# Dividing three early loads of a DMA-bound transpose into pieces of 112, 8 and 8 partitions

## The chip, the cores and the metric

One core of one Trainium2 chip. The metric is the device time of one execution in microseconds, and less is better. All runs told here are of the fast or undisturbed state.

## The reference

```python
def setup_inputs():
    return {"x": np.random.randn(8192, 8192).astype(np.float32)}

def reference(x):
    return np.transpose(x)
```

268 MB have to be read from HBM and as many written. There is no arithmetic.

## The kernel before

The input is read in 135 loads of 128 rows, one row to a partition, most of them 16 KB to a row (2 MB). TensorE transposes 128x128 blocks into PSUM, ScalarE and VectorE copy them into wide register strips in SBUF (`regs`), and finished strips go out in 142 stores. ScalarE's queue issues the loads, SyncE's queue the stores. These are the parts that matter here:

```python
    EARLY = NR          # 8: the first eight loads have buffers of their own
    SLOTS = [1, 0, 2]   # later loads take turns in three buffers
    ...
        def load(t):
            s, q = active[t][0]
            j0 = s * J + q * R
            i0 = t % CH * P
            nc.scalar.dma_start(
                out=home(t), in_=x[i0:i0 + P, j0:j0 + len(active[t]) * R]
            ).then_inc(s_early[t] if t < EARLY else s_ld[slot(t)], 16)
    ...
        def transposes(t):
            if t < EARLY:
                nc.tensor.wait_ge(s_early[t], 16)
            else:
                nc.tensor.sem_inc(s_ld[slot(t)], -16).wait_op(s_ld[slot(t)], 16, "sem-ge")
            ...   # 128x128 transposes into two halves of PSUM
    ...
        for t in range(EARLY):
            load(t)
        ...       # copies of tile t out of PSUM, then
            if t in loads_after:
                nc.scalar.wait_ge(s_pe, n)
                load(loads_after[t])
    ...
                src = regs[:, base:base + B * rows]
                st = wide_dma(nc, nc.sync, "qSPDynamicHW", dst, src)   # one store
                st.then_inc(s_st[w["reg"]], 16)
```

## Time and profile before

| | before |
|---|---|
| median of three runs | 1266.98 us (1266.64 to 1268.45) |
| profiled span | 1265.6 us |
| moved | 537 MB, 424 GB/s over the span |
| busiest compute engine | TensorE, 58% |
| end of the last packet of most DMA engines, of the last one | 1258.0 us, 1263.9 us |

The prediction shows the busy table and most of the windows. Two more pieces are needed for the comparison. The first is the row of the page with the rate in 40 equal slices of the kernel before:

```profile
GB/s 384 418 430 430 429 429 429 431 429 430 430 428 430 429 429 430 430 430 428 425 424 411 428 430 430 427 427 430 430 430 430 430 428 429 428 431 427 427 422 323
```

The second is three stretches of its start, in the view by windows (stretch, length, then PE, PEld, DVE, ACT and POOL busy with their counts, granted clock, DMA share, GB/s):

```profile
20.00:30.00 10.00, 8.12 (x66) 7.80 (x65) 2.98 (x2) 4.56 (x3) 0.00 (x0) 1.00 1.01 434
30.00:40.00 10.00, 7.04 (x52) 6.72 (x52) 4.58 (x2) 3.03 (x4) 0.00 (x0) 0.93 1.00 419
60.00:80.00 20.00, 12.97 (x84) 12.30 (x82) 6.03 (x5) 5.15 (x7) 0.00 (x0) 0.83 1.00 429
```

The last two columns are the ones to keep: the share of the sixteen DMA engines' time in which they have a packet, and what they moved. Here they go together, share 1.0 and about 430 GB/s.

A word on packets. The trace has a record of every DMA packet with its queue, start, duration and size. A packet of a load is one partition's row. The views do not list packets one by one; where I quote their durations I counted them from these records. They do not name the engine.

### The profile page before, as it was taken

What the parts mean: (1) busy time and instruction counts of PE and PEld (TensorE: products, weight loads), DVE (VectorE), ACT (ScalarE), POOL (GpSimd) and SP (SyncE); (2) the same over time, 40 slices, a digit from 0 to 9 for tenths busy, and PEclk for the clock granted to TensorE, in tenths of its full rate; (3) what the DMA queues carried; (4) which work ended last, traced back from release to release, by engine and by line L of the source; (5) the groups of instructions that cost most, each with busy time, mean ns of one, the idle gap of its engine ahead of it and who ended that gap; (6) DMA issues with size and microseconds to landing.
All of it is one profiled execution on the core that took longest, in us unless ns stands there. A gap on an engine that the chain in (4) does not pass through costs nothing. (4 is left out here: it accounts for less than half of the span.)

```text
span 1265.6 us, 9771 instructions
## 1 busy us (share of the span) xinstructions
PE 737.3 (58%) x4096; PEld 698.5 (55%) x4096; DVE 294.1 (23%) x223; ACT 254.8 (20%) x291; POOL 0.7 (0%) x6
## 2 busy tenths in 40 slices
PE   6565655646656475665456656556565565555651
PEld 6555655646555465555455546456464565555651
DVE  2222222222222222122122222222222222232220
ACT  3121211212112121122111212122121221212221
POOL 0000000000000000000000000000000000000000
PEclk9777786877768777677877777867778777777775
DMA  9999999999999999999999999999999999999997
GB/s 384 418 430 430 429 429 429 431 429 430 430 428 430 429 429 430 430 430 428 425 424 411 428 430 430 427 427 430 430 430 430 430 428 429 428 431 427 427 422 323
DMA packets 40283, 537.00 MB, mean 424 GB/s; under 512 B 4432, under 2 KB 4432, under 8 KB 7248
## 3 DMA queue, kind: packets, MB, share of 16 engines
q1 hardware_dynamic: 20832, 268.44, 50.0%
q10 hardware_dynamic: 19440, 268.44, 49.9%
q8 instruction: 3, 0.05, 0.0%
q14 instruction: 8, 0.07, 0.0%
HBM read 268.44 MB, written 268.44 MB: 424 GB/s over the span
## 5 line engine op out<-in xcount | busy, mean ns | idle before, releaser
L194 PE MATMUL ps<-ident,in 128*128 128x128 f32 x4048 | 731.2, 359 | 505.4 <-PEq L190 500.1
L194 PEld LDWEIGHTS ps<-ident,in 128*128 128x128 f32 x4048 | 692.5, 219 | 543.5 <-issue 542.6
L260 DVE COPY regs<-ps 128x1024 f32<-128x1024 f32 (+3 forms) x223 | 294.1, 1354 | 933.5 <-PE ps L194 482.5
L260 ACT COPY regs<-ps 128x512 f32<-128x512 f32 (+3 forms) x290 | 253.6, 934 | 983.5 <-DMA out_dram<-regs 548.5
L194 PE MATMUL ps<-ident,regs 128*128 128x128 f32 x32 | 4.1, 285 | 0.8 <-PEq L190 0.8
L194 PEld LDWEIGHTS ps<-ident,regs 128*128 128x128 f32 x32 | 3.9, 209 | 1.0 <-issue 1.0
L260 ACT ACT_TABLE_LOAD x1 | 1.3, 1283 | 5.7 <-issue 5.7
L194 PE MATMUL ps<-ident,extra 128*128 128x128 f32 x16 | 2.2, 289 | 0.0
L194 PEld LDWEIGHTS ps<-ident,extra 128*128 128x128 f32 x16 | 2.1, 208 | 0.1
L163 POOL TENSOR_SCALAR_AFFINE_SELECT ident<-ident 128x128 f32<-128x128 f32 x1 | 0.3, 292 | 0.2 <-POOL ident L161 0.2
L161 POOL MEMSET ident<- 128x128 f32 x1 | 0.2, 205 | 0.5 <-SPq L127 0.5
L319 POOL MEMSET const-bfloat16-1.0<- 128x1 bf16 x1 | 0.1, 101 | 0.0
L319 POOL MEMSET const-uint8-127<- 128x1 uint8 x1 | 0.1, 101 | 0.0
L319 POOL MEMSET const-float32-0.0<- 128x1 f32 x1 | 0.1, 98 | 0.2 <-issue 0.2
L319 POOL MEMSET const-float32-1.0<- 128x1 f32 x1 | 0.1, 98 | 0.0
## 6 DMA issues: line engine op xcount, KB each, us to landing
in<-in_x_dram ACTq DMA_DIRECT2D x120, 2048.0 KB, 18.4
out_dram<-regs SPq DMA_DIRECT2D x114, 2048.0 KB, 18.8
out_dram<-regs SPq DMA_DIRECT2D x4, 1792.0 KB, 21.6
out_dram<-regs SPq DMA_DIRECT2D x4, 1536.0 KB, 20.0
out_dram<-regs SPq DMA_DIRECT2D x4, 1280.0 KB, 18.7
out_dram<-regs SPq DMA_DIRECT2D x4, 1024.0 KB, 20.3
in<-in_x_dram ACTq DMA_DIRECT2D x2, 1792.0 KB, 20.6
in<-in_x_dram ACTq DMA_DIRECT2D x2, 1536.0 KB, 17.7
```

What stands on the lines that cost most here:

```text
L161: nc.gpsimd.memset(ident, 0.0).then_inc(s_id, 1)
L163: nc.gpsimd.affine_select(out=ident, in_=ident, compare_op=mybir.AluOpType.not_equal, fill=1.0, base=0, pattern=[[-1, P]], channel_multipl ...
L194: tr = nc.tensor.transpose(pss[h][:, k * P:(k + 1) * P], src[:, j:j + R - B + 1:B], ident,)
L260: cp = nc.scalar.copy(out=o, in_=i) if h == 0 else nc.vector.tensor_copy(out=o, in_=i)
L319: nc = _bacc.Bacc("TRN2", target_bir_lowering=False, num_devices=1)
```

## The change

Loads 8, 9 and 10 (`EARLY` to `EARLY + 2`) are each cut into partitions 0-111, 112-119 and 120-127. The intent is that the first piece goes to sixteen DMA engines, seven rows each, and the two small ones to the same eight engines, one row each. Then eight engines carry nine rows and the others seven, and the halves run out of step. Here the eight with nine rows are called the lower ones, the others the upper ones.

```diff
+        def cuts(t):
+            return [(0, 112), (112, P - 8), (P - 8, P)] if t in (EARLY, EARLY + 1, EARLY + 2) else [(0, P)]
+
         def load(t):
             ...
-            nc.scalar.dma_start(
-                out=home(t), in_=x[i0:i0 + P, j0:j0 + len(active[t]) * R]
-            ).then_inc(s_early[t] if t < EARLY else s_ld[slot(t)], 16)
+            for p0, p1 in cuts(t):
+                nc.scalar.dma_start(
+                    out=home(t)[p0:p1], in_=x[i0 + p0:i0 + p1, j0:j0 + len(active[t]) * R]
+                ).then_inc(s_early[t] if t < EARLY else s_ld[slot(t)], 16)
             ...
-                nc.tensor.sem_inc(s_ld[slot(t)], -16).wait_op(s_ld[slot(t)], 16, "sem-ge")
+                landed = 16 * len(cuts(t))
+                nc.tensor.sem_inc(s_ld[slot(t)], -landed).wait_op(s_ld[slot(t)], landed, "sem-ge")
             ...
-        first = EARLY + (full[-1] + 1 - EARLY) % NIN
+        first = EARLY + NIN + (full[-1] + 1 - EARLY) % NIN
```

The last line only unrolls three more tiles on TensorE, because those wait for another number.

## The prediction

"Port" in this text is a place where rows might hold each other up. The sum came to 1266 us for a slow engine among the upper eight and to 1271.8 for one among the lower, weighed 60 to 40 to 1268. Its term c, 4 us out of 0 to 11, was the author's guess. The 2.4 us a row behind the 11 us had no trace behind them then, but the runs show such rows: the slowest load packet of the changed kernel from 20 to 80 us took 2351 ns, and in e7_one_load those that start at 33 us have a median of 2442 ns, against 611 before.

> **What bounds the kernel now.** I read the engines' busy table first, because it rules things out.
>
> ```profile
> PE 737.3 (58%) x4096; PEld 698.5 (55%) x4096; DVE 294.1 (23%) x223; ACT 254.8 (20%) x291; POOL 0.7 (0%) x6
> ```
>
> No compute engine is busy for more than 58% of the 1265.6 us span. Then the row of the slices for the DMA engines and the two queues:
>
> ```profile
> DMA  9999999999999999999999999999999999999997
> ...
> DMA packets 40283, 537.00 MB, mean 424 GB/s; under 512 B 4432, under 2 KB 4432, under 8 KB 7248
> ...
> q1 hardware_dynamic: 20832, 268.44, 50.0%
> q10 hardware_dynamic: 19440, 268.44, 49.9%
> ```
>
> Every slice but the last is full, and loads (q10) and stores (q1) take half each. The kernel moves 268.44 MB in and as much out, and cannot move less. So the question is only the rate, which I took from the view by windows (columns: PE, PEld, DVE, ACT, POOL busy with counts, granted clock, DMA share, GB/s):
>
> ```profile
> 0.00:10.00 10.00, 4.52 (x19) 3.77 (x20) 1.22 (x1) 1.87 (x2) 0.70 (x6) 1.00 0.78 273
> 10.00:20.00 10.00, 7.66 (x57) 7.27 (x56) 2.98 (x2) 3.30 (x2) 0.00 (x0) 1.00 1.02 435
> 40.00:60.00 20.00, 9.50 (x54) 9.34 (x53) 2.29 (x1) 3.44 (x6) 0.00 (x0) 0.69 1.01 418
> 400.00:600.00 200.00, 119.32 (x652) 111.78 (x650) 49.98 (x53) 40.32 (x55) 0.00 (x0) 0.74 1.01 429
> 600.00:800.00 200.00, 114.73 (x656) 109.60 (x656) 46.51 (x29) 39.76 (x46) 0.00 (x0) 0.78 1.01 425
> 1250.00:1260.00 10.00, 0.00 (x0) 0.00 (x0) 0.00 (x0) 0.00 (x0) 0.00 (x0) 0.50 0.81 338
> 1260.00:1265.60 5.60, 0.00 (x0) 0.00 (x0) 0.00 (x0) 0.00 (x0) 0.00 (x0) 0.50 0.05 20
> ```
>
> The reader is to see a plateau of about 430 GB/s, a poor first 10 us, small dents at 40 to 60 and at 600 to 800 us, and a tail of some 8 us where few engines still move data. The waits agree: the copies out of PSUM wait most for stores to land and free a register strip, so compute is paced by the DMA.
>
> ```profile
> ACT regs L260 <- DMA out_dram<-regs: 548.5, 55, 21.0
> DVE regs L260 <- PE ps L194: 482.5, 72, 14.4
> DVE regs L260 <- DMA out_dram<-regs: 451.0, 57, 12.3
> ```
>
> The trace's single packet records say more than these views. A packet is one partition's row; a full one is 16 KB and takes 611 ns (load) or mostly 615 ns (store). Joining records end to start over 300 to 360 us gives sixteen serial streams, one per DMA engine: fourteen need 610.0 ns for 16 KB, one 610.8, and one 613.6. Each engine moves 33.55 MB, that is 2048 full packets, so the slow one should lose 2048 x 3.6 ns = 7.4 us. It does about that: the spread of the sixteen semaphore increments of one DMA grows from 2.3 us at 260 us to 4.2 us at 600 us with one engine alone falling behind, and at the end the bulk of the engines is done by 1258.1 us while one goes on to 1263.9 us. So the finish is set by one slow DMA engine, 5.8 us behind the bulk. The reported 1266.98 us is 3.1 us more than that last packet.
>
> [...]
>
> **The change part by part.** Bytes: none added or removed. It touches loads 8, 9 and 10 (2 MB each, landing at 31.8, 37.8 and 44.1 us). Each engine had 8 rows of each. [...] Over three loads that is 3 rows more, 3 x 0.610 = +1.8 us for a lower engine and -1.8 us for an upper one; the halves are then 3.7 us apart.
>
> Issues: six more on ScalarE's queue, at 0.33 us each by the three present ones in the timeline:
>
> ```profile
> 16.81 0.33 ACTq L156 DMA_DIRECT2D in<-in_x_dram  x1
> 21.52 0.33 ACTq L156 DMA_DIRECT2D in<-in_x_dram  x1
> 26.22 0.33 ACTq L156 DMA_DIRECT2D in<-in_x_dram  x1
> ```
>
> 2 us in all, but each load is issued 14.7 to 17.5 us before it lands, with three loads ahead of it in the ring, so this is hidden: 0. Semaphore packets: 8 more per piece, 16 per load, 48 in all at 9 ns over 16 engines: 0. TensorE: it waits for 48 instead of 16, and its loop begins one round (3 tiles) later; its 4096 transposes and their order stay, and it is not the bound: 0.
>
> Later landing: load 8 waits for a ninth row on the lower half, +0.6 us, load 9 +1.2, load 10 +1.8 to 2.3. TensorE gets tiles 8 to 10 that much later. The rings do not run dry for it: at an issue in the steady state the load ring still has 4.2 us for its first-finishing engine and the store ring 5.6 us (issue and landing times of the trace at 118 to 156 us), and the new offset is 3.7 us. It is taken out of a reserve that suffices, barely. Cost: 0 to 1 us.
>
> Port sharing, the term I am least sure of: [...] a row takes up to 4 x 0.61 = 2.4 us [...], 1.8 us more than alone; six pieces give up to 6 x 1.8 = 11 us on the lower engines. [...] I take 0 to 11 us, most likely about 4.
>
> What out-of-step can save: the dents at 54 to 58 and at 671 to 678 us, where all engines run loads almost alone and load packets take 700 to 1600 ns. Their excess, summed over packets and divided by 16, is 0.6 and 1.2 us. At most 1.8 us; I take 1.
>
> Sum for the end. If the slow engine is an upper one: it ends at 1263.9 - 1.8 = 1262.1, a lower one at 1258.1 + 1.8 + port cost c = 1259.9 + c. With c = 4 the end is 1263.9, with the 1 us saved 1262.9; plus 3.1 gives 1266. If it is a lower one: 1263.9 + 1.8 + 4 - 1 + 3.1 = 1271.8. I hold upper for a little likelier (the intent is to load the lower half more), 60 to 40: 1268.
>
> **The rivals.**
> First, the pure relief of the slow engine: it is in the upper half, [...]c = 0. Then 1262.1 + 3.1 - 1 = 1264 us. For it: the single engine that ends last[...].
> Second, port sharing in full: c = 11, end 1270.9 + 3.1 = 1274 us with an upper slow engine, 1279 with a lower one. [...] against: stores fill in between, and the 4 KB packets of the first store, which is split another way, mostly took their usual 165 ns.
> Third, a starved ring: the offset (3.7 us plus c) exceeds the 4.2 us reserve of the load ring, so the upper half idles. That costs nothing while the lower half is the bound; it would matter only if waiting spread to the lower half, at the block change of 610 to 680 us, where a load was already issued into an empty ring. I give it 2 to 5 us more.
> Fourth, a better rate for the whole run, because halves out of step mix reads and writes more evenly. Loads 7 and 8, which run alone, land 4.9 us apart, 611 to 612 ns for each of the eight packets of an engine; the mix has 610. Alone or mixed is the same, so I see no room here. Against it too: the sixteen engines are already spread over 1 to 2 us. Each 0.1% of the plateau would be 1.2 us.
>
> **Range and chances.** The plateau forbids a large gain: 2048 packets x 610 ns = 1249.3 us of pure transfer, plus 2 us before the first packet and 3.1 after the last, make 1254; 2% faster would be 1241.6. Over 2% slower would be 1292.3, a loss of 25 us, over twice the full port term. Predicted 1268 us, from 1262.5 (relief, no port cost) to 1276 (slow lower engine with moderate port cost, or full port cost with an upper one). Faster 0.01, same 0.97, slower 0.02.
>
> **What would show it.** Rows per engine: q10 should have 48 more packets, 19488, and 4480 under 512 B. Half and half: the increments of load 10's pieces, and of later loads, should fall in two groups of eight, 3.7 us apart or more. Port cost: load packets at 27 to 45 us far over 611 ns, about 48 of them near 2.4 us; if none is, c = 0. Slow engine: if the last packet ends earlier than 1263.9 us, it was an upper one. Saved dents: fewer load packets over 700 ns at 54 to 58 and 671 to 678 us. I am wrong if the plateau leaves 429 to 430 GB/s, or if a wait of the loads for their ring shows DMA share under 1 between 60 and 1240 us.

## The result, and the profile after

The changed kernel takes 1283.5 us (median of four runs, 1282.59 to 1286.35), the one before 1267.34 in the same rounds. The ratio is 1.0131, 95% interval 1.0112 to 1.0149. A ratio is always the mean time of one kernel's fast runs over that of the other's of the same rounds, so it is not quite the ratio of the medians. It is 16 us slower, outside my range of 1262.5 to 1276.

From the page of the changed kernel, the rows of the slices, the packets and the load queue:

```profile
DMA  9999999999999999999999999999999999999997
GB/s 352 271 413 428 429 429 430 431 428 430 429 431 428 431 429 428 430 428 430 425 423 389 429 430 429 430 428 430 431 429 430 427 429 429 429 429 429 429 421 317
DMA packets 40331, 537.00 MB, mean 419 GB/s; under 512 B 4480, under 2 KB 4480, under 8 KB 7296
...
q10 hardware_dynamic: 19488, 268.44, 50.2%
```

The DMA row is the same as before, all nines. The rate is the same to within 3 GB/s in 35 of the 40 slices. It is far lower in the first three (352, 271, 413 against 384, 418, 430) and lower at the change of column blocks (389 against 411) and in the tail (317 against 323). The same place in the view by windows, columns as above:

```profile
20.00:30.00 10.00, 6.82 (x55) 6.50 (x54) 2.98 (x2) 3.73 (x2) 0.00 (x0) 1.00 1.03 352
30.00:40.00 10.00, 2.63 (x22) 2.46 (x22) 2.29 (x1) 1.93 (x2) 0.00 (x0) 0.86 1.00 192
40.00:60.00 20.00, 11.14 (x64) 10.79 (x63) 4.58 (x2) 1.93 (x2) 0.00 (x0) 0.81 1.01 280
60.00:80.00 20.00, 10.13 (x63) 10.00 (x64) 2.29 (x1) 3.98 (x6) 0.00 (x0) 0.66 0.99 399
80.00:100.00 20.00, 10.10 (x68) 9.43 (x66) 4.71 (x4) 5.78 (x6) 0.00 (x0) 0.91 1.01 430
...
600.00:800.00 200.00, 113.47 (x640) 108.12 (x640) 46.53 (x31) 38.99 (x47) 0.00 (x0) 0.74 1.00 421
```

Between 30 and 40 us the DMA share is 1.00 and the rate 192 GB/s. The engines are not waiting for work; each packet takes longer. This is the first thing to learn here: a full DMA row says that packets are under way, not that they are quick.

The sum: against 430 GB/s the four stretches from 20 to 80 us lack 78 x 10 + 238 x 10 + 150 x 20 + 31 x 20 = 6780 KB, 15.8 us at 430. The kernel before lacks 330 KB there, 0.8 us. That leaves 15.0 us. From 600 to 800 us 421 instead of 425 GB/s is another 1.9 us. Together 16.9, and the spans differ by 17.0 (1282.6 against 1265.6). The two parts differ in kind. At the start the share stays at 1. At the change of column blocks it falls. The deepest ten microseconds there, of the kernel before and then of the changed one, where it comes ten microseconds later:

```profile
670.00:680.00 10.00, 7.56 (x45) 7.47 (x46) 1.52 (x1) 3.85 (x4) 0.00 (x0) 0.66 0.98 369
...
680.00:690.00 10.00, 4.50 (x20) 4.16 (x21) 2.29 (x1) 1.93 (x2) 0.00 (x0) 0.50 0.84 331
```

There the engines of the changed kernel do wait for work: from 670 to 690 us about 1.4 us averaged over them, from 660 to 700 us 1.3 us more than before. Little else changed: from the packet records, most engines finish at 1274.7 instead of 1258.0 us and the last one at 1280.9 instead of 1263.9, so the slow last engine is 6 us behind as before.

The packets agree. I sum what each packet took above the usual duration of its size (over 25 ns more) and divide by 16 engines. From 20 to 80 us that is 0.7 us before and 15.3 us after. 437 load packets over 700 ns stand against 32.

The compute engines follow. From the timeline of the changed kernel (start, duration, queue, line, operation, operands, count), the issues of the three loads and of the second store (its line is joined with the third):

```profile
17.47 1.26 ACTq L163 DMA_DIRECT2D in<-in_x_dram  x3
21.51 1.04 ACTq L163 DMA_DIRECT2D in<-in_x_dram  x3
26.22 1.04 ACTq L163 DMA_DIRECT2D in<-in_x_dram  x3
...
44.47 24.37 SPq L28 DMA_DIRECT2D out_dram<-regs  x2
```

The three loads' issues, three pieces each, take 1.0 to 1.3 us and still come long before their data, at nearly the same times as before (16.81, 21.52 and 26.22 us). So the issuing is not the matter. The second store goes out at 44.47 us, 9 us later than before (35.33): the tiles reach TensorE late.

### The profile page after: what moved, and what is told of

Same layout as the page of the kernel before. It is cut to its first block, busy times and chain, and to the rows that moved or that the text cites. A ratio compares the mean times of both kernels' runs of the same rounds, so it can differ in the third digit from the quotient of the medians.

```text
span 1282.6 us, 9775 instructions
## 1 busy us (share of the span) xinstructions
PE 730.0 (57%) x4096; PEld 689.7 (54%) x4096; DVE 294.1 (23%) x223; ACT 254.9 (20%) x291; POOL 0.7 (0%) x6
## 2 busy tenths in 40 slices
DMA packets 40331, 537.00 MB, mean 419 GB/s; under 512 B 4480, under 2 KB 4480, under 8 KB 7296
## 3 DMA queue, kind: packets, MB, share of 16 engines
q10 hardware_dynamic: 19488, 268.44, 50.2%
## 5 line engine op out<-in xcount | busy, mean ns | idle before, releaser
L202 PE MATMUL ps<-ident,in 128*128 128x128 f32 x4048 | 723.2, 356 | 528.3 <-PEq L198 524.1
L202 PEld LDWEIGHTS ps<-ident,in 128*128 128x128 f32 x4048 | 682.8, 218 | 568.0 <-issue 566.9
```

The source lines that it names most:

```text
L202: tr = nc.tensor.transpose(pss[h][:, k * P:(k + 1) * P], src[:, j:j + R - B + 1:B], ident,)
```

## The experiments

The theory was that rows which different engines move at once hold each other up, and that it depends on their partitions: neighbouring ones do so more than evenly spread ones. The expectations call it the port theory. The rivals were the offset itself (halves out of step starve a ring or stall TensorE), the number of pieces, and addresses in HBM. Twelve kernels ran, in three groups, each group compared with runs of the kernel before on the same chip. The second group shares seven of its eight such runs with the first.

| run | what is done to loads 8, 9, 10 (or other) | median us | before | ratio (95%) | packet excess, 20 to 80 us |
|---|---|---|---|---|---|
| the change | 112, 8, 8 | 1283.5 | 1267.3 | 1.0131 (1.0112-1.0149) | 15.3 us |
| e1_skew_spread | offset by added loads, partitions four apart | 1272.67 | 1268.29 | 1.0036 (1.0020-1.0053) | 0.9 |
| e2_skew_two_ports | the same on neighbouring partitions | 1275.34 | 1268.29 | 1.0051 (1.0034-1.0068) | 4.4 |
| e3_halves | 0-63, 64-127 | 1281.6 | 1268.29 | 1.0100 (1.0083-1.0117) | 13.8 |
| e4_even_odd | evens, odds | 1267.61 | 1268.29 | 0.9995 (0.9978-1.0012) | 0.7 |
| e9_offset_free_ports | 64 evens, 48 odds, 8, 8 | 1279.24 | 1268.23 | 1.0081 (1.0064-1.0098) | 10.7 |
| e5_source_rows | the change, other HBM rows | 1283.22 | 1268.23 | 1.0118 (1.0101-1.0135) | 13.7 |
| e6_112_16 | 112, 16 | 1279.61 | 1268.23 | 1.0083 (1.0066-1.0100) | 12.0 |
| e10_late_skew | added loads near 1040 us | 1273.89 | 1268.23 | 1.0052 (1.0032-1.0072) | 1.1 |
| e7_one_load | the change on load 8 only | 1276.02 | 1269.05 | 1.0056 (1.0039-1.0073) | 6.8 |
| e11_split_in_steady_state | the change on loads 40 to 42 | 1276.13 | 1269.05 | 1.0053 (1.0036-1.0070) | 0.9 (7.1 at 80 to 600) |
| e12_quarters | four times 32, four apart | 1268.26 | 1269.05 | 1.0003 (0.9987-1.0020) | 0.7 |
| e14_offset_strided | loads 8, 9: 64, 32, four times 8, strided | 1273.05 | 1269.05 | 1.0035 (1.0018-1.0051) | 3.5 |

All gave the right result but e5_source_rows. Its output is wrong, which doesn't matter for the time.

### Halves against even and odd

```diff
-            return [(0, 112), (112, P - 8), (P - 8, P)] if t in (...) else [(0, P)]
+            return [(0, 64), (64, P)] if t in (...) else [(0, P)]                  # e3_halves
+            # e4_even_odd: home(t)[0:127:2] and home(t)[1:128:2], the same steps in x
```

> Loads 8, 9 and 10 as partitions 0-63 and 64-127: 16 engines each, 4 rows an engine, no engine has more than another. Port theory: [...]rows take twice 611 ns where all engines are in the same piece: 8 rows x 0.61 x 3 loads = +14.7 us, less what engines in different pieces save: 1274 to 1283. Offset theory (imbalance): 1267, as before. A theory that 7 rows per engine make a bad pattern of HBM addresses: 1267 too.

> Loads 8, 9 and 10 as even and odd partitions: the same counts, sizes, engines and semaphores as the halves[...]. Port theory: at most half of the loss of the halves, 1267 to 1273, depending on which rows an engine is given. If only the number of pieces matters: the same as the halves.

These two differ in nothing but which partitions stand together: two pieces of 64 rows, four rows to an engine (64 over sixteen; the share is 0.97 and 1.01 at 30 to 40 us), the same bytes, semaphores and issues. The windows from 30 to 40 and 40 to 60 us of the halves:

```profile
30.00:40.00 10.00, 4.54 (x27) 4.38 (x26) 2.29 (x1) 1.93 (x2) 0.00 (x0) 0.67 0.97 209
40.00:60.00 20.00, 10.14 (x61) 9.79 (x59) 4.58 (x2) 1.93 (x2) 0.00 (x0) 0.84 1.01 301
```

and of the even and odd ones:

```profile
30.00:40.00 10.00, 7.28 (x58) 6.95 (x58) 4.58 (x2) 3.61 (x4) 0.00 (x0) 1.00 1.01 418
40.00:60.00 20.00, 7.86 (x54) 7.51 (x52) 2.44 (x2) 3.08 (x6) 0.00 (x0) 0.74 1.02 422
```

209 against 418 GB/s: half. The halves lose 13.3 us without any piece of 8, and the even and odd pieces lose nothing. The median load packet at 28 us takes 1276 ns in the halves and 611 in the evens and odds. This settles that a balanced split can cost nearly as much as the change, and that the choice of partitions decides. (The rows that go with the evens and the odds also lie further apart in HBM; the run with other rows of HBM below separates the two.)

### Four quarters, strided

```diff
+            return [(a, P, 4) for a in range(4)] if t in (...) else [(0, P, 1)]     # start, end, step
```

> Loads 8, 9 and 10 each as four pieces of 32 partitions four apart; [...]two rows an engine, one piece more than the change has. Port theory: within 2 us of before[...]. If pieces with few rows per engine, or many pieces, are slow by themselves: +8 us or more.

It is as fast as before (1.0003). Four pieces, more than the change has, with two rows to an engine (32 over sixteen; the share is 1.00 at 30 to 40 us), cost nothing. So neither the number of pieces nor the few rows an engine.

### Other rows of HBM

```diff
-                    out=home(t)[p0:p1], in_=x[i0 + p0:i0 + p1, j0:...]
+                    out=home(t)[p0:p1], in_=x[i0 + 3 * p0:i0 + 3 * p1 - 2:3, j0:...]
```

> The change, but loads 8, 9 and 10 read every third row of the input (a row pitch of 96 KB instead of 32): another pattern of addresses in HBM, the same partitions. The result is wrong on purpose. Port theory[...]: as the change, +14 to +17 us. A theory that rows in blocks of seven meet in HBM: clearly different from the change, by over 4 us.

+15 us, as the change. With three times the row pitch in HBM and the same partitions the loss stays. So the pitch of the source rows is not its cause, and a wider pitch alone doesn't take the loss away, as the even and odd pieces or the quarters do.

### The offset alone

e1_skew_spread and e2_skew_two_ports leave the loads whole and add four small ones behind each, into a buffer that is no longer used:

```diff
+            if EARLY <= t < EARLY + 3:
+                for d in range(4 * (t - EARLY), 4 * (t - EARLY) + 4):
+                    a = d % 4 + 32 * (d // 4 % 2) + 64 * (d // 8); b = a + 29; c = 4   # e1: four apart
+                    # e2: a = 8 * d; b = a + 8; c = 1                                    # neighbours
+                    nc.scalar.dma_start(out=extra[a:b:c], in_=x[i0 + a:i0 + b:c, j0:j0 + 2048]).then_inc(s_dummy, 16)
```

> The kernel before, with four loads of 8 partitions x 8 KB into a spent buffer behind each of loads 8, 9 and 10, on partitions four apart, so that the eight lower DMA engines get 2 full rows more per load, 6 in all (the offset of the change, 3.7 us)[...]. Port theory[...]: 0 to +3.7 us over before, 1267 to 1271, no load packet over 700 ns at 27 to 50 us beyond those of before. Offset theory (the halves out of step starve the rings or stall TensorE): most of the change's +16 us, 1279 to 1284. It also tells the half of the slow engine: 0 if it is an upper one, +3.7 us if a lower one.

> The same with the twelve added loads on 8 neighbouring partitions each[...]. Same bytes, engines and count as the spread one. Port theory: their 8 KB packets take up to four times 316 ns, 1.2 us, so the lower engines lose up to 12 x 0.95 = 11 us more than with spread partitions; 1272 to 1284. Offset theory and a theory of the number of pieces: the same time as the spread one, within 1 us.

The spread ones cost 4.4 us by the medians, close to the 3.7 us of work that they add to the lower engines, and not the change's 16. At 1272.7 us it is still 1.7 us over the range of the port theory. Their 8 KB packets take 309 to 342 ns throughout. The stated sign failed: from 27 to 50 us 30 load packets take over 700 ns, against 5 before; in sum the packet excess is still only 0.2 us more than before (0.9 against 0.7). The ones on neighbouring partitions cost 2.7 us more. That is a miss in size: I had expected up to 11, from rows four times as long (the slowest row of the changed kernel, 2351 ns against 611, is 3.8 times). The records tell where it sits. Behind load 8, where all engines arrive within a microsecond and no store is out, the 8 KB packets take up to 1058 ns and the first 16 KB packets of the next load up to 1760. Behind loads 9 and 10, where 4 KB store packets stand between, every 8 KB packet takes 309 to 313 ns, but the 16 KB load packets that run at the same time take up to 1532 and 1212 ns. Against the spread run the packet excess is 1.8 us more behind load 8, 0.8 behind load 9 and 1.2 behind load 10. So the delay is there each time, and behind loads 9 and 10 it stands in packets other than the added ones. Why it stays so far under 11 us isn't shown.

### The offset on other partitions, two tries

```diff
+  # e9_offset_free_ports, loads 8 to 10 (start, end, step)
+  [(0, P, 2), (1, 96, 2), (97, P, 4), (99, P, 4)]
+  # e14_offset_strided, loads 8 and 9
+  [(0, P, 2), (1, P, 4)] + [(3 + 32 * b, 32 + 32 * b, 4) for b in range(4)]
```

> The change's own intent with other partitions: loads 8, 9 and 10 as 64 even partitions, 48 odd ones (1 to 95) and two pieces of 8 partitions four apart (97 to 125, 99 to 127). Lower engines 4+3+1+1 = 9 rows, upper 7, the same offset of 6 rows, one piece more per load[...]. Port theory: 1267 to 1273 (at most the +3.7 us of the lower engines and some meetings in the 48-row piece). Offset theory (halves out of step are slow by themselves): as the change, 1280 to 1285.

> [...]loads 8 and 9 as 64 even partitions, 32 partitions four apart, and four pieces of 8 partitions four apart; lower engines 10 rows, upper 6, so an offset of 8 rows (4.9 us) after two loads against 6 in the change. Port theory and a slow engine in the lower half: +2.4 to +5 us. Offset theory: over +12.

The first is a failed test: +11 us, 1279.2, is outside the range of the port theory and just under that of the offset theory. The packets put at least part of it elsewhere. The 64 evens of load 8 run at 611 ns. Only then, in the piece of 48 odd partitions, three rows to an engine if sixteen share them evenly, do all take about 1180 to 1250 ns. So that piece was not free of delays as I had supposed; how its rows are dealt to the engines, I don't know. Three rows at these durations are about 1.7 us too many on each engine, so three such pieces are about 5 us, half of the run's excess. The other half lies in later rows of loads 8 to 10, which mostly took 700 to 1300 ns as well. It isn't explained. The second try uses only pieces that had proved quick, and makes a larger offset, 8 rows: +4.0 us. The increments of the first store to land show two groups (eight engines within 2.2 us, eight 5.1 to 5.7 us after the first), so the offset is real there, and it doesn't cost 12 us. Beside that stand 2.4 us more work on the lower engines and 2.8 us of packet excess over before, 1.5 of it from 30 to 34 us, when the lower engines are at the pieces of 8 and the upper ones at the next load. That rows of the two hold each other up there, and that the two terms overlap in part, is an inference.

### Which piece: 112 and 16, and one load only

```diff
+  [(0, 112), (112, P)] if t in (EARLY, EARLY + 1, EARLY + 2)                 # e6_112_16
+  [(0, 112), (112, P - 8), (P - 8, P)] if t == EARLY                         # e7_one_load
```

> Loads 8, 9 and 10 as 112 and 16 partitions: every engine has 7 + 1 rows, no half carries more[...]. Port theory: like the change, +10 to +16 us. Offset theory: as before, 0 to +2 us.

> The change on load 8 alone. Port theory: the loss belongs to the packets of the split loads, so about a third of +16 us: +4 to +7. If the halves, once out of step, kept slowing later loads: more than half of it, over +8.

112 and 16 costs 11.4 us with an equal number of rows meant for every engine. So most of the loss, 11.4 of 16 us, is there without the pieces of 8 that make the imbalance. One load alone costs 7.0 us, somewhat over a third of 16, at the edge of what I expected. It is the cleanest picture, because load 9 behind it is a whole one again. These are the durations of the 16 KB load packets by the microsecond in which they start, over all engines (ns):

| start, us | before: least, median, most | one load: least, median, most |
|---|---|---|
| 28 | 611, 611, 619 | 1015, 1041, 1242 |
| 30 | 611, 615, 619 | 1004, 1021, 1092 |
| 33 | 611, 613, 709 | 2408, 2442, 2499 |
| 34 | 608, 611, 805 | 2113, 2149, 2382 |
| 35 | 611, 611, 618 | 1942, 1985, 2033 |
| 39 | 611, 611, 611 | 611, 611, 614 |

From 26 to 31 us the piece of 112 runs: no packet is quicker than 989 ns. From about 32 to 37 us the two small pieces run. The median of the packets that start at 33 us is 2442 ns, and 4 x 611 = 2444: as if four rows took turns. What they would take turns at, the records don't show. The point is the least value. From 32.1 to 37.0 us 43 load packets start, and the small pieces have 16 rows, so at least 27 of the 43 are rows of the next, whole load. Yet none of the 43 takes less than 1.13 us, and from 33 us on none less than 1.69. The upper eight engines have none of the 16 rows, only rows of the whole load, and by 39 us such rows take 611 ns again. So the small pieces slow engines that have no row of them. By 39 us, when the small pieces are through, everything is back at 611.

So one load costs: seven rows at about 1050 ns instead of 611, 3.1 us on every engine, and about three more packet times at 2.4, 2.0 and 1.1 us on every engine, 5.5 instead of 1.8, 3.7 us. Together 6.8 us, which is the excess in the table above (the kernel before has 0.7 of it too). The kernel is bound by the DMA engines, so it should go into the time about one to one: 7.0 measured.

### Later, where stores are many

```diff
+  [(0, 112), (112, P - 8), (P - 8, P)] if t in (40, 41, 42)     # and more tiles unrolled on TensorE
```

> The same three cuts on loads 40, 41 and 42, near 330 us, where 16 KB store packets stand between the load packets and the engines are 2 us apart. Port theory: [...]+3 to +10 us. If the loss came from the start (tiles late for TensorE while few stores are out): 0 to +2.

Three windows of it, 320 to 380 us, where the kernel before has 428, 428 and 431 GB/s:

```profile
320.00:340.00 20.00, 12.77 (x64) 11.41 (x63) 4.71 (x4) 3.79 (x3) 0.00 (x0) 0.67 1.01 397
340.00:360.00 20.00, 7.45 (x40) 6.99 (x39) 4.58 (x2) 1.93 (x2) 0.00 (x0) 0.67 1.00 384
360.00:380.00 20.00, 11.97 (x64) 11.62 (x62) 2.47 (x2) 3.85 (x4) 0.00 (x0) 0.62 1.01 401
```

+7.1 us, a little under half of the early loss, at a DMA share of 1.00. Why it is less there isn't shown. The loss is not a matter of the start and of TensorE waiting for its first tiles. (A first build of this kernel was refused in the check for a race, because its TensorE loop still waited for 16; unrolling more tiles mended it.)

### Which half has the slow engine

e10_late_skew is e1's edit with `if T - 24 <= t < T - 21`.

> The kernel before, with the same twelve loads of 8 partitions four apart as in the spread skew, but behind three loads near 1030 to 1060 us, past the last place where rings run dry before the end. The lower engines get 3.7 us more work. If the engine that ends last is a lower one: +3.0 to +4.5 us. If it is an upper one: 0 to +1 us, since the lower ones have 5.8 us to spare.

+5.7 us by the medians, over the upper end of what I had named for a lower engine (the last packets also have 2.7 us more excess there than before). The packet records decide it better than the time. The four 8 KB loads behind the first of the three are 32 packets, four on each of the eight lower engines. 28 of them start from 1034.1 to 1038.1 us, and four alone, one after the other, from 1040.4 to 1044.4. The same comes again behind the second: four alone from 1055.8 to 1059.8. That is the engine that runs 6 us behind, and it has such packets. So it is one of the lower eight.

## Why the prediction was wrong

What bounds the kernel was right: the plateau stayed at 429 to 430 GB/s, and no compute engine came near the path. That gains over 2% are impossible, and the class of within 2%, followed from it.

The number of engines was right. q10 has 19488 packets and 4480 are under 512 B, the numbers predicted: 48 more, which is 8 for each of the six pieces of 8. The added loads of 8 rows show up on eight engines too: in e10_late_skew one engine has four of the 32 packets of four such loads.

The issues of ScalarE and the semaphores cost nothing, as predicted.

The step that failed is "Port sharing, the term I am least sure of". That rows hold each other up was right, though where they do isn't shown; how much it costs, and whom it holds up, was not: "I take 0 to 11 us, most likely about 4". It measured 14.6 us of packet excess (15.3 less the 0.7 of before). The sign for it failed in the same way: of the "about 48" load packets near 2.4 us at 27 to 45 us there are 10 over 2.2 us, but 219 take over 700 ns. Two things were left out. First, I charged the two small pieces only. The piece of 112 costs about 3 us a load too (3.1 in the run of one load): I had counted its rows at 611 ns, which the kernel before shows for whole loads alone. Second, I charged the lower engines only, so that the upper ones and the slow one could hide part of it. In the run of one load every engine slows towards the pace of the slowest rows (none under 1.69 us from 33 to 37 us, the slowest 2.5). A loss of all sixteen engines can't be hidden.

"If the slow engine is an upper one", 60 to 40: wrong, it is a lower one. My own rule for that case with c = 14.6 gives 1263.9 + 1.8 + 14.6 + 3.1 = 1283.4, without the saving. That is what was measured, though the agreement to a tenth is luck: the packets above also show 1.9 us at the change of blocks that this sum doesn't have.

"What out-of-step can save", 1 us: not there. The excess at 600 to 700 us was 1.4 us before and 1.75 after, and a dry moment at 680 us came to 1.4 us, averaged over the engines. The halves came out of step, but did not stay so. In the first store to land after the cut, eight engines stand within 1.0 us and the other eight follow at 2.8 to 4.5, the two groups that I had named; from 83 us on all sixteen lie in one spread of 3.4 us, without a gap. The rival of a starved ring doesn't explain the start: the DMA share stays at 1 from 20 to 60 us. But the sign that the prediction gave for being wrong, a share under 1 between 60 and 1240 us, did come at the change of blocks, the place that this rival named: 0.84 from 680 to 690 us, against 0.98 in that dent before. It is worth about 1.4 us, under the "2 to 5 us" given for it. Whether the halves' offset caused it isn't shown; the balanced halves have a dry moment there too (0.7 us from 660 to 700 us), 112 and 16 has none.

What stays open is how the rows of a piece of 112 or 48 are dealt to the engines. The durations, about 1050 and 1200 ns on all engines, say that rows hold each other up; the records don't name engines, so I can't say which. No version here beats the kernel before. Even and odd pieces and quarters equal it. The slow engine is among the eight that the pieces of 8 go to (it has four of 32 packets behind each of two loads in e10_late_skew), so it can't be relieved in this way.

## What to carry to other kernels

In a kernel whose DMA engines are full, keep loads of 128 partitions whole. If they must be cut, the cuts that cost nothing here were every second partition (64) and every fourth (32), at 611 ns a row. A stride alone is no safeguard: 48 odd partitions took about 1200 ns a row. A cut into neighbouring partitions cost 2.4 to 7 us for each 2 MB load here, wherever it stood. Read the rate beside the share: a DMA share of 1.00 with half the usual GB/s means slow packets, and the packets' durations name the place. When one engine is held up at a shared resource, ask first whether the others can go on, before hiding its delay behind them.
